# An RMSNorm-and-projection kernel: work put into the engine queues by planned times, with another load order at the start

## The chip, the cores and the metric

The kernel runs on one core of a Trainium2 chip. Its engines are TensorE (PE in the profile, with its weight loads as PEld), VectorE (DVE), ScalarE (ACT), GpSimd (POOL) and SyncE (SP), which here only issues transfers; 16 DMA engines move the data. Each engine takes its own instructions in program order. The metric is the device time of one execution in microseconds; lower is better.

## The reference

```python
# x: 8 x 1024 x 768, gamma: 768, w_qkv: 768 x 2304, all float32
rms = np.sqrt(np.mean(x ** 2, axis=-1, keepdims=True) + eps)
x_norm = x / rms * gamma
return np.matmul(x_norm, w_qkv).astype(np.float32)
```

The 8 x 1024 rows of x make 64 row tiles of 128. The output is 8192 x 2304 in float32, 75.5 MB.

## The kernel before, in words

The row factor 1/rms commutes with the product, so the kernel multiplies the raw x (as bf16) with gamma-scaled weights (as bf16) and scales each row when a result leaves PSUM. A row tile goes through: a load of 128x768 float32 (`load_x`), a cast to bf16 on VectorE (`cast_x`, L96), a transpose to the layout that TensorE wants (xT, six blocks of 128x128), the sum of squares and the square root on ScalarE (`stat`, L101 and L103) with the reciprocal on VectorE (L105), and then products. One product unit (`unit`) is six matmuls, one for each block of 128 of the 768, over up to 512 output columns into one PSUM bank, and one eviction with the row scale, on VectorE (L129) or ScalarE (L131). A full tile has units of 512, 512, 512, 512 and 256 columns: 30 matmuls and 6 x 2304 = 13,824 columns streamed.

The program has two phases.

The **head** covers row tiles 0 to 5 (`HEAD`), while the weights still arrive in nine slices of 256 columns (`load_w`, `conv_w`). The list `order` (L138) gives the order both of the loads and of the work. When a tile comes, it is cast, transposed on TensorE (`trans_pe`, L110, the two halves copied out of PSUM by VectorE L113 and ScalarE L114) and multiplied with the slices that are there; when a slice comes, its six blocks are scaled and converted by VectorE (L88) and ScalarE (L91) in turn, and all tiles that are there are multiplied with it. Code order is queue order: the conversion of the next slice stands on VectorE and ScalarE behind all evictions of the slice before it. None of the six output tiles is stored before the head's last unit is in the queues, because the stores (`store`, L134, whole rows of 2304 columns) are issued by SyncE after the loads and after the first two DMA transposes.

The **main loop** covers tiles 6 to 63. At the top of tile t it loads tile t + 6, casts tile t + 2, transposes it by DMA (`trans_dma`, L118) and takes its statistics; then come the five units of tile t and the store of its whole output. So SyncE's queue repeats: x load, transpose, store. The load of gamma is issued by ScalarE's queue behind the load of an activation table; ten matmuls on a zero tile (L150) stand on TensorE behind the transpose of gamma (L146).

Of the kernel before, what the change touches and what calls it, by code (L numbers as in the profile page):

```python
# [9 lines left out]
HEAD = 6  # L10

XBAR = True
CW = 256
# [3 lines left out]
def kernel(  # L17
# [8 lines left out]
    nc = tc.nc  # L26
# [9 lines left out]
    assert K == Kw  # L36
# [4 lines left out]
    NC = N // CW  # L41
    inv_k = 1.0 / float(K)

    singles = ctx.enter_context(tc.tile_pool(name="singles", bufs=1))
    wst = ctx.enter_context(tc.tile_pool(name="wst", bufs=NC))
# [5 lines left out]
    outp = ctx.enter_context(tc.tile_pool(name="outp", bufs=HEAD))  # L51
# [4 lines left out]

    ident_f = singles.tile([P, P], f32)
# [3 lines left out]
    eps_sb = singles.tile([P, 1], f32)  # L61
    nc.vector.memset(eps_sb, float(eps))
    warm = singles.tile([P, NT], bf16)
    nc.gpsimd.memset(warm, 0.0)

    tbl = singles.tile([P, 1], f32)
    nc.scalar.activation(out=tbl, in_=eps_sb, func=AF.Sqrt)  # L67

    g6 = singles.tile([KO, P], f32)
# [4 lines left out]
    X, XB, XT, RS, OUT, WF = {}, {}, {}, {}, {}, {}  # L74
# [5 lines left out]
    def load_w(c):  # L80
        WF[c] = wst.tile([P, KO, CW], f32, name="w_f")
        nc.sync.dma_start(out=WF[c], in_=wv[:, :, c * CW:(c + 1) * CW])

    def conv_w(c):
        for ko in range(KO):
            o = w_b[:, ko, c * CW:(c + 1) * CW]
            if ko % 2 == 0:
                nc.vector.tensor_scalar(out=o, in0=WF[c][:, ko, :], scalar1=g_sb[:, ko:ko + 1],  # L88
                                        scalar2=None, op0=mult)
            else:  # L90
                nc.scalar.activation(out=o, in_=WF[c][:, ko, :], func=AF.Copy,  # L91
                                     scale=g_sb[:, ko:ko + 1], bias=0.0)
# [5 lines left out]
    def stat(t):  # L98
# [5 lines left out]
        RS[t] = stats.tile([P, 1], f32, name="rstd")  # L104
        nc.vector.reciprocal(out=RS[t], in_=rms)  # L105

    def trans_pe(t):
        pt = psum_t.tile([P, KO, P], bf16, name="pt")
        for ko in range(KO):
            nc.tensor.transpose(out=pt[:, ko, :], in_=XB[t][:, ko * P:(ko + 1) * P], identity=ident)  # L110
# [9 lines left out]
    def unit(t, n0, nl, eng):  # L120
        pm = psum_mm.tile([P, NT], f32, name="pm")
        for ko in range(KO):
            nc.tensor.matmul(out=pm[:, :nl], lhsT=XT[t][:, ko, :], rhs=w_b[:, ko, n0:n0 + nl],  # L123
                             start=(ko == 0), stop=(ko == KO - 1))
        if t not in OUT:
            OUT[t] = outp.tile([P, N], f32, name="ot")
        o = OUT[t][:, n0:n0 + nl]
        if eng:
# [4 lines left out]
    def store(t, n0=0, nl=N):  # L133
        nc.sync.dma_start(out=of[t * P:(t + 1) * P, n0:n0 + nl], in_=OUT[t][:, n0:n0 + nl])  # L134
# [3 lines left out]
    order = [("x", 0), ("w", 0), ("x", 1), ("x", 2), ("w", 1), ("x", 3), ("w", 2),  # L138
             ("x", 4), ("x", 5)] + [("w", c) for c in range(3, NC)]
    load_x(0)  # L140
    nc.scalar.dma_start(out=g6, in_=gamma.rearrange("(ko p) -> ko p", p=P))
    for kind, i in order[1:]:
        (load_x if kind == "x" else load_w)(i)

    g_ps = psum_t.tile([P, KO], f32, name="pt")
    nc.tensor.transpose(out=g_ps, in_=g6, identity=ident_f[:KO, :KO])  # L146
    nc.vector.tensor_copy(out=g_sb, in_=g_ps)  # L147
    wps = psum_mm.tile([P, NT], f32, name="pm")
    for _ in range(10):
        nc.tensor.matmul(out=wps, lhsT=ident, rhs=warm, start=True, stop=True)  # L150

    xs, ws = [], []
    flip = 0
    for kind, i in order:
        if kind == "x":
            cast_x(i)
            trans_pe(i)
            stat(i)
            xs.append(i)
            todo = [(i, c) for c in ws]  # L160
        else:
            conv_w(i)
            ws.append(i)
            todo = [(t, i) for t in xs]
        for t, c in todo:
            unit(t, c * CW, CW, flip)
            flip ^= 1


    AHEAD = 2  # L170
    trans = trans_dma if XBAR else trans_pe
    for t in range(HEAD, min(HEAD + 6, MT)):
        load_x(t)
    for t in range(HEAD, min(HEAD + AHEAD, MT)):
        cast_x(t)
        trans(t)
        stat(t)
    for t in range(HEAD):
        store(t)
    n_tiles = [(i, min(NT, N - i)) for i in range(0, N, NT)]  # L180
    for t in range(HEAD, MT):
        a = t + AHEAD
        if t + 6 < MT:
            load_x(t + 6)
        if a < MT:
            cast_x(a)
            if XBAR:
                trans(a)
            stat(a)
        for i, (n0, nl) in enumerate(n_tiles):  # L190
            unit(t, n0, nl, i % 2 == 0)
            if i == 2 and a < MT and not XBAR:
                trans(a)
            if t == MT - 1:
                store(t, n0, nl)
# [37 lines left out]
```

## Time and profile before

| | us |
|---|---|
| runs shown | 434.64, 432.77, 434.39 (median 434.39) |
| the profiled execution | 435.1 |
| its span, from the first to the last instruction | 433.2 |
| TensorE busy in the span | 394.3 |
| VectorE busy, ScalarE busy, GpSimd busy | 175.6, 179.2, 1.2 |
| mean granted TensorE clock, as a share | 0.984 |

The span is 1.9 us shorter than the profiled execution's own time. The profile cuts the span into 40 slices of 10.8 us and gives each engine's busy share in tenths. A matmul's end is modelled and matmuls overlap, so TensorE's pace is read from starts, not from busy time. An entry of the chain of waits is one piece of the path that ended last: its start, its length, and what it was.

### The profile page before, as it was taken

The numbers are of one execution on the slowest core, as the hardware profiler recorded it, in microseconds if no ns is written. First come the engines' busy times: TensorE is split into PE (matmuls) and PEld (weight loads), VectorE is DVE, ScalarE is ACT, GpSimd is POOL, SyncE is SP. The second block draws the span as 40 slices with busy tenths as digits, with TensorE's granted clock in tenths as the row PEclk, the third lists the DMA queues.
The fourth block names the chain that finished last, engine by engine and source line by source line (L and its number), as shares of the span: only waits on it lengthen the run. The fifth ranks groups of instructions, "written<-read, shape, count | busy, mean of one in ns | idle before, by whom it ended". The sixth has DMA issues, their size and how long they took to land.

```text
span 433.2 us, 5483 instructions
## 1 busy us (share of the span) xinstructions
PE 394.3 (91%) x2076; PEld 208.7 (48%) x2111; DVE 175.6 (41%) x365; ACT 179.2 (41%) x370; POOL 1.2 (0%) x7
## 2 busy tenths in 40 slices
PE   3576888667999999999999999999999999999996
PEld 1344666232555555455555545555554555555453
DVE  1324444231444443444444344444434444443432
ACT  1445555330444443344344334434433443443431
POOL 1000000000000000000000000000000000000000
PEclk9999999696999999999999999999999999999999
DMA  8991000799999999999999999999999999999775
GB/s 299 359 368 65 3 0 2 281 402 357 291 313 286 302 305 300 310 315 314 292 295 308 301 305 314 311 279 313 304 301 309 313 307 294 300 306 300 248 244 218
DMA packets 72501, 119.50 MB, mean 276 GB/s; under 512 B 48662, under 2 KB 55708, under 8 KB 64412
## 3 DMA queue, kind: packets, MB, share of 16 engines
q1 hardware_dynamic: 72464, 119.16, 88.9%
q8 instruction: 16, 0.26, 0.2%
q14 instruction: 9, 0.07, 0.0%
q10 hardware_dynamic: 12, 0.00, 0.0%
HBM read 32.25 MB, written 75.50 MB: 249 GB/s over the span
## 4 chain that ended last, share of the span: by engine, by line
PE 87%; DMA 5%; DVE 3%; ACT 3%; issue 1%; DVEq 0%; ACTq 0%
PE pm L123 85%; DMA xT<-xb 4%; DVE ot L129 1%; DMA g<-in_gamma_dram 1%; ACT sq L101 1%; PE pm L150 1%; PE pt L110 1%; ACT xT L114 1%; DVE w_b L88 1%; DVE xT L113 1%; DVE xb L96 0%; ACT rms L103 0%; ACT L67 0%; ACT ot L131 0%; DVE rstd L105 0%
## 5 line engine op out<-in xcount | busy, mean ns | idle before, releaser
L123 PE MATMUL pm<-w_b,xT 128*128 128x512 bf16 (+1 forms) x2029 | 385.7, 350 | 24.3 <-DMA xT<-xb 10.6
L123 PEld LDWEIGHTS <-xT 128*128 128x128 bf16 x2064 | 204.0, 99 | 205.2 <-issue 12.5
L129 DVE TENSOR_SCALAR ot<-pm,rstd 128x512 f32<-128x512 f32 (+1 forms) x201 | 128.1, 638 | 213.6 <-PE pm L123 208.4
L131 ACT ACTIVATE ot<-pm,rstd 128x512 f32<-128x512 f32 (+1 forms) x143 | 92.5, 647 | 228.0 <-PE pm L123 226.8
L101 ACT ACTIVATE sq<-x_t 128x768 bf16<-128x768 f32 x64 | 53.3, 834 | 0.0
L96 DVE CAST xb<-x_t 128x768 bf16<-128x768 f32 x64 | 35.2, 549 | 0.0
L105 DVE RECIPROCAL rstd<-rms 128x1 f32<-128x1 f32 x64 | 10.5, 164 | 25.8 <-ACT rms L103 25.7
L103 ACT ACTIVATE rms<-ssq,eps_sb 128x1 f32<-128x1 f32 x64 | 18.8, 294 | 2.1
L101 ACT ACTIVATION_READ_ACCUMULATOR sq<-x_t 128x1 f32 x64 | 12.2, 191 | 0.0
L91 ACT ACTIVATE w_b<-w_f,g_sb 128x256 bf16<-128x256 f32 x27 | 11.6, 496 | 0.0
L114 ACT COPY xT<-pt 128x384 bf16<-128x384 bf16 x6 | 2.9, 480 | 19.9 <-DVE xT L113 19.9
L110 PE MATMUL pt<-ident,xb 128*128 128x128 bf16 x36 | 4.3, 280 | 4.2 <-DVE xb L96 4.2
L88 DVE TENSOR_SCALAR w_b<-w_f,g_sb 128x256 bf16<-128x256 f32 x27 | 7.8, 345 | 0.0
L146 PE MATMUL pt<-ident_f,g 6*128 6x6 f32 x1 | 0.2, 238 | 7.1 <-DMA g<-in_gamma_dram 7.1
L110 PEld LDWEIGHTS <-xb 128*128 128x128 bf16 x36 | 3.2, 127 | 6.4 <-DVE xb L96 5.7
L113 DVE COPY xT<-pt 128x384 bf16<-128x384 bf16 x6 | 2.1, 358 | 8.6 <-PE pt L110 8.6
L150 PE MATMUL pm<-warm,ident 128*128 128x512 bf16 x10 | 4.4, 628 | 0.0
L146 PEld LDWEIGHTS pt<-ident_f,g 6*128 6x128 f32 x1 | 0.2, 178 | 7.1 <-issue 7.1
L147 DVE COPY g_sb<-pt 128x6 f32<-128x6 f32 x1 | 0.2, 166 | 5.5 <-PE pt L146 5.5
L150 PEld LDWEIGHTS <-ident 128*128 128x128 bf16 x10 | 1.3, 140 | 2.3 <-issue 2.2
L67 ACT ACT_TABLE_LOAD x1 | 1.3, 1283 | 0.7 <-PEq L214 0.7
L60 DVE CAST ident<-ident_f 128x128 bf16<-128x128 f32 x1 | 0.5, 511 | 1.3 <-POOL ident_f masks.py:199 1.3
(9 smaller groups left out, 1.7 us busy)
## 6 DMA issues: line engine op xcount, KB each, us to landing
out_dram<-ot SPq DMA_DIRECT2D x63, 1152.0 KB, 5.4
x_t<-in_x_dram SPq DMA_DIRECT2D x64, 384.0 KB, 6.1
w_f<-in_w_qkv_dram SPq DMA_DIRECT2D x9, 768.0 KB, 10.6
out_dram<-ot SPq DMA_DIRECT2D x4, 256.0 KB, 2.8
xT<-xb SPq DMA_TRANSPOSE x58, 6.3
out_dram<-ot SPq DMA_DIRECT2D x1, 128.0 KB, 1.9
g<-in_gamma_dram ACTq DMA_DIRECT2D x1, 3.0 KB
```

The lines of the kernel that those rows point to most:

```text
L88: nc.vector.tensor_scalar(out=o, in0=WF[c][:, ko, :], scalar1=g_sb[:, ko:ko + 1], scalar2=None, op0=mult)
L91: nc.scalar.activation(out=o, in_=WF[c][:, ko, :], func=AF.Copy, scale=g_sb[:, ko:ko + 1], bias=0.0)
L96: nc.vector.tensor_copy(out=XB[t], in_=X[t])
L101: nc.scalar.activation(out=sq, in_=X[t], func=AF.Square, accum_out=ssq)
L103: nc.scalar.activation(out=rms, in_=ssq, func=AF.Sqrt, scale=inv_k, bias=eps_sb)
L105: nc.vector.reciprocal(out=RS[t], in_=rms)
L110: nc.tensor.transpose(out=pt[:, ko, :], in_=XB[t][:, ko * P:(ko + 1) * P], identity=ident)
L114: nc.scalar.copy(out=XT[t][:, h:, :], in_=pt[:, h:, :])
L123: nc.tensor.matmul(out=pm[:, :nl], lhsT=XT[t][:, ko, :], rhs=w_b[:, ko, n0:n0 + nl], start=(ko == 0), stop=(ko == KO - 1))
L129: nc.vector.tensor_scalar(out=o, in0=pm[:, :nl], scalar1=RS[t], scalar2=None, op0=mult)
L131: nc.scalar.activation(out=o, in_=pm[:, :nl], func=AF.Copy, scale=RS[t], bias=0.0)
L150: nc.tensor.matmul(out=wps, lhsT=ident, rhs=warm, start=True, stop=True)
```

## The change

Instead of issuing instructions as the code runs, the new program collects calls with a planned time (`at`) and issues them sorted by it. The planned time of a unit is when a running sum of matmul time says TensorE reaches it; the casts, transposes, statistics, evictions and stores get times around it. The sorted order is each engine's queue; the hardware still waits for data by semaphores, not by the planned times.

- Head: loads come in the order w x x x w x x w x w w w. The weight slices are 256, 256, 256, 512, 512 and 512 columns wide, and the third holds columns 2048 to 2303. Two buffers serve the slices of 512, so the third of them waits for the conversion of the first.
- A slice's six blocks are converted by VectorE, ScalarE and GpSimd in turn, two each.
- The load of gamma is the first instruction of the program on ScalarE's queue; the zero tile is set by VectorE; eight warm-up matmuls stand ahead of gamma's transpose and use the zero tile for both operands.
- The reciprocal is a step of its own (`recip`). The whole transposed tile is copied out of PSUM by VectorE (`copy_xT`).
- Tiles 6 to 11 are transposed on TensorE, in the stream of the tile before; DMA transposes begin with tile 12, planned 7.5 us ahead of the tile's first unit.
- The output tile is two buffers, columns 0 to 1023 and 1024 to 2303, seven of each; each half is stored as soon as it is full, in the head too. The last tile is still stored unit by unit. Evictions alternate between VectorE and ScalarE over the whole program.

```diff
-HEAD = 6
-XBAR = True
-CW = 256
+ARRIVALS = "wxxxwxxwxwww"
+C0 = [0, 256, 2048, 512, 1024, 1536]
+CHUNKS = [256, 256, 256, 512, 512, 512]
+FIRST_XBAR = 12
+WARM = 8
...
+    PARTS = [(0, 1024), (1024, N - 1024)]
...
-    outp = ctx.enter_context(tc.tile_pool(name="outp", bufs=HEAD))
+    outp = ctx.enter_context(tc.tile_pool(name="outp", bufs=7))
...
+    g6 = singles.tile([KO, P], f32)
+    nc.scalar.dma_start(out=g6, in_=gamma.rearrange("(ko p) -> ko p", p=P))
...
+        WF[c] = wst.tile([P, KO, n], f32, name=f"w_f{n}", bufs=3 if n == 256 else 2)
...
-            if ko % 2 == 0:
...
+            if ko % 3 == 0:
+                nc.vector.tensor_scalar(out=o, in0=i, scalar1=g, scalar2=None, op0=mult)
+            elif ko % 3 == 1:
+                nc.scalar.activation(out=o, in_=i, func=AF.Copy, scale=g, bias=0.0)
             else:
...
+                nc.gpsimd.tensor_scalar(out=o, in0=i, scalar1=g, scalar2=1.0, op0=mult, op1=mult)
...
+    def copy_xT(t):
         XT[t] = xTp.tile([P, KO, P], bf16, name="xT")
-        h = KO // 2
-        nc.vector.tensor_copy(out=XT[t][:, :h, :], in_=pt[:, :h, :])
-        nc.scalar.copy(out=XT[t][:, h:, :], in_=pt[:, h:, :])
+        nc.vector.tensor_copy(out=XT[t], in_=PT[t])
...
+    def store(t, h, n0, nl):
+        p0 = PARTS[h][0]
+        nc.sync.dma_start(out=of[t * P:(t + 1) * P, n0:n0 + nl], in_=OUT[t, h][:, n0 - p0:n0 - p0 + nl])
...
+    def at(time, fn, *args):
+        plan.append((time, len(plan), fn, args))
...
+            nc.tensor.matmul(out=wps, lhsT=warm[:, :P], rhs=warm, start=True, stop=True)
+
+    US = 6 * 0.2158 / 512
...
+    def unit(t, n0, nl, ready=0.0):
+        s = max(state["pe"], ready)
+        state["pe"] = e = s + nl * US
+        at(s, mm, t, n0, nl)
+        state["flip"] ^= 1
+        at(e + 0.2, evac, t, n0, nl, state["flip"])
+        h = part(n0)
+        left[t, h] = left.get((t, h), PARTS[h][1]) - nl
+        if t == MT - 1:
+            at(e + 0.9, store, t, h, n0, nl)
+        elif left[t, h] == 0:
+            at(e + 1.4, store, t, h, *PARTS[h])
+
+    at(0.0, warm_up)
+    at(3.0, gamma_in)
...
+            now += 1.02
+            at(now, cast_x, t)
+            at(now + 0.6, trans_pe, t)
+            at(now + 1.0, copy_xT, t)
+            at(now + 0.1, stat, t)
+            at(now + 1.6, recip, t)
...
+                unit(t, C0[c], CHUNKS[c], now + 1.7)
...
     for t in range(HEAD, MT):
...
+        T = state["pe"]
+        at(T - 15, load_x, t)
+        if t < FIRST_XBAR:
+            at(T - 4.5, cast_x, t)
+            at(T - 3.0, trans_pe, t)
+            at(T - 2.5, copy_xT, t)
+        else:
+            at(T - 8.5, cast_x, t)
+            at(T - 7.5, trans_dma, t)
+        at(T - 5, stat, t)
+        at(T - 3, recip, t)
+        for n0, nl in n_tiles:
+            unit(t, n0, nl)
+
+    for _, _, fn, args in sorted(plan, key=lambda p: p[:2]):
+        fn(*args)
```

VectorE at the start, before (xb_148 and xb_182 are the casts of tiles 0 and 1; w_f_106 is the first weight slice):

```order
L113 COPY xT_157<-pt_150 128x384
L105 RECIPROCAL rstd_165<-rms_163 128x1
L88 TENSOR_SCALAR w_b_102<-w_f_106,g_sb_101 128x256 x3
L96 CAST xb_182<-x_t_108 128x768
L113 COPY xT_191<-pt_184 128x384
L105 RECIPROCAL rstd_199<-rms_197 128x1
L129 TENSOR_SCALAR ot_208<-pm_201,rstd_199 128x256
```

VectorE at the start, after (xb_146, xb_162 and xb_187 are the casts of tiles 0, 1 and 2; w_f256_104 and w_f256_112 are the first two slices):

```order
L94 TENSOR_SCALAR w_b_103<-w_f256_104,g_sb_102 128x256 x2
L102 CAST xb_146<-x_t_106 128x768
L124 COPY xT_160<-pt_153 128x768
L102 CAST xb_162<-x_t_108 128x768
L114 RECIPROCAL rstd_169<-rms_151 128x1
L124 COPY xT_185<-pt_171 128x768
L102 CAST xb_187<-x_t_110 128x768
L146 TENSOR_SCALAR ot0_194<-pm_178,rstd_169 128x256
L114 RECIPROCAL rstd_196<-rms_167 128x1
L124 COPY xT_212<-pt_198 128x768
L114 RECIPROCAL rstd_216<-rms_192 128x1
L94 TENSOR_SCALAR w_b_103<-w_f256_112,g_sb_102 128x256 x2
```

The first slice's conversion moved ahead of the first cast, and the casts of tiles 1 and 2 ahead of the first eviction.

TensorE at the start, after: the end of tile 1's transpose (xb_162), the first unit, and the beginning of tile 2's transpose (xb_187). Before, the first unit stood directly behind the transpose of tile 0.

```order
L120 MATMUL pt_153<-ident_100,xb_146 128x128
L120 LDWEIGHTS xb_162
L120 MATMUL pt_171<-ident_100,xb_162 128x128
...
L133 LDWEIGHTS xT_160
L133 MATMUL pm_178<-w_b_103,xT_160 128x256
...
L120 LDWEIGHTS xb_187
L120 MATMUL pt_198<-ident_100,xb_187 128x128
```

The first unit moved behind the transposes of two tiles.

SyncE in the steady part, before: two turns of the loop (x_t is the load of tile t + 6, xT the transpose of tile t + 2, ot the store of tile t).

```order
L78 DMA x_t_1344<-in_x_dram 128x768
L118 DMA_TRANSPOSE xT_1348<-xb_1346 128x6x128
L134 DMA out_0_dram<-ot_1364 128x2304
L78 DMA x_t_1399<-in_x_dram 128x768
L118 DMA_TRANSPOSE xT_1403<-xb_1401 128x6x128
L134 DMA out_0_dram<-ot_1419 128x2304
```

SyncE in the steady part, after (ot0 is the first half of an output tile, ot1 the second half of the same tile; the transpose between them is that of the tile two behind it):

```order
L83 DMA x_t_1193<-in_x_dram 128x768
L152 DMA out_0_dram<-ot0_1191 128x1024
L128 DMA_TRANSPOSE xT_1217<-xb_1205 128x6x128
L152 DMA out_0_dram<-ot1_1215 128x1280
L83 DMA x_t_1250<-in_x_dram 128x768
L152 DMA out_0_dram<-ot0_1248 128x1024
L128 DMA_TRANSPOSE xT_1274<-xb_1262 128x6x128
L152 DMA out_0_dram<-ot1_1272 128x1280
```

The transpose moved from behind an x load and a whole store to behind the store of half a tile, and nearer to the tile that needs it.

## Rows read from the trace of the kernel before

**Rows 1.** The page: busy time by engine, then tenths in 40 slices.

```profile
PE 394.3 (91%) x2076; PEld 208.7 (48%) x2111; DVE 175.6 (41%) x365; ACT 179.2 (41%) x370; POOL 1.2 (0%) x7
...
PE   3576888667999999999999999999999999999996
...
GB/s 299 359 368 65 3 0 2 281 402 357 291 313 286 302 305 300 310 315 314 292 295 308 301 305 314 311 279 313 304 301 309 313 307 294 300 306 300 248 244 218
```

**Rows 2.** Chain of waits, steady part: start us, us, what.

```profile
131.03 9.46 PE pm L123 x49
...
160.20 9.46 PE pm L123 x49
```

**Rows 3.** Chain of waits, start, loop entry and end.

```profile
1.91 5.07 DMA g<-in_gamma_dram
...
76.38 2.85 DMA xT<-xb
...
86.50 14.01 DMA xT<-xb
...
429.90 0.48 DVE ot L129
```

**Rows 4.** Timeline of TensorE, head and loop entry: start us, us, what [idle before].

```profile
14.96 1.44 PE L123 MATMUL pm<-w_b,xT 128*128 128x256 bf16 x6 [2.60 <-DVE w_b L88]
...
24.52 3.79 PE L123 MATMUL pm<-w_b,xT 128*128 128x256 bf16 x17 [0.34 <-ACT w_b L91]
29.35 0.82 PE L110 MATMUL pt<-ident,xb 128*128 128x128 bf16 x6 [1.04 <-DVE xb L96]
...
34.20 2.87 PE L123 MATMUL pm<-w_b,xT 128*128 128x256 bf16 x24 [0.84 <-DVE w_b L88]
38.12 0.51 PE L110 MATMUL pt<-ident,xb 128*128 128x128 bf16 x6 [1.05 <-DVE xb L96]
...
71.19 4.18 PE L123 MATMUL pm<-w_b,xT 128*128 128x256 bf16 x36 [0.84 <-DVE w_b L88]
...
100.56 9.68 PE L123 MATMUL pm<-w_b,xT 128*128 128x512 bf16 x36 [6.66 <-DMA xT<-xb]
```

**Rows 5.** Windows: busy us by engine, then PEclk, DMA share, GB/s.

```profile
103.00:106.00 3.00, 3.00 (x10) 1.14 (x9) 0.75 (x1) 0.27 (x1) 0.00 (x0) 0.60 1.10 376
106.00:109.00 3.00, 3.00 (x19) 1.62 (x18) 0.77 (x2) 1.10 (x3) 0.00 (x0) 1.00 1.12 354
```

**Rows 6.** The first x load: issue time, then landing.

```profile
L78 SPq DMA_DIRECT2D x_t<-in_x_dram x1: 402/402/402, 0.7 to 0.7; - x1
...
DMA to landing us min/median/max: 3.1/3.1/3.1
```

**Rows 7.** The first weight load: issue time, then landing.

```profile
L82 SPq DMA_DIRECT2D w_f<-in_w_qkv_dram x1: 419/419/419, 1.2 to 1.2; - x1
...
DMA to landing us min/median/max: 5.1/5.1/5.1
```

**Rows 8.** Groups by shape: xcount | busy us, mean ns | idle before.

```profile
L129 DVE TENSOR_SCALAR ot<-pm,rstd 128x512 f32<-128x512 f32 x116 | 87.0, 750 | 120.5 <-PE pm L123 115.6 <-DMA out_dram<-ot 4.9
...
L129 DVE TENSOR_SCALAR ot<-pm,rstd 128x256 f32<-128x256 f32 x85 | 41.1, 484 | 93.1 <-PE pm L123 92.7
L96 DVE CAST xb<-x_t 128x768 bf16<-128x768 f32 x64 | 35.2, 549 | 0.0
...
L88 DVE TENSOR_SCALAR w_b<-w_f,g_sb 128x256 bf16<-128x256 f32 x27 | 7.8, 345 | 0.0
...
L113 DVE COPY xT<-pt 128x384 bf16<-128x384 bf16 x6 | 2.1, 358 | 8.6 <-PE pt L110 8.6
```

**Rows 9.** Timeline of GpSimd at the start.

```profile
1.01 0.29 POOL masks.py:199 TENSOR_SCALAR_AFFINE_SELECT ident_f<-ident_f 128x128 f32<-128x128 f32 x1
```

**Rows 10.** Timeline of SyncE, steady part.

```profile
203.80 2.59 SPq L118 DMA_TRANSPOSE xT<-xb  x1
```

**Rows 11.** The tile xT between 150 and 200 us.

```profile
DMA to landing us min/median/max: 6.2/6.5/8.5
```

More of the change, by code (lines that the diff above doesn't have):

```diff
@@ L35 @@
     Kw, N = w_qkv.shape
-    assert K == Kw
+    assert K == Kw and sum(CHUNKS) == N
     P = 128
@@ L55 @@
     ctx.enter_context(tc.manual_schedule())
+    g6 = singles.tile([KO, P], f32)
+    nc.scalar.dma_start(out=g6, in_=gamma.rearrange("(ko p) -> ko p", p=P))
+    eps_sb = singles.tile([P, 1], f32)
+    nc.vector.memset(eps_sb, float(eps))
+    warm = singles.tile([P, NT], bf16)
+    nc.vector.memset(warm, 0.0)
+    tbl = singles.tile([P, 1], f32)
+    nc.scalar.activation(out=tbl, in_=eps_sb, func=AF.Sqrt)
     ident_f = singles.tile([P, P], f32)
@@ L131, in unit @@
             nc.scalar.activation(out=o, in_=pm[:, :nl], func=AF.Copy, scale=RS[t], bias=0.0)
[L133 to L154, printed above, removed]
-        if kind == "x":
[L156 to L160, printed above, removed]
-        else:
[L162 to L167, printed above, removed]
@@ L170 @@
[L170 to L179, printed above, removed]
+    def store(t, h, n0, nl):
+        p0 = PARTS[h][0]
+        nc.sync.dma_start(out=of[t * P:(t + 1) * P, n0:n0 + nl], in_=OUT[t, h][:, n0 - p0:n0 - p0 + nl])
+    plan = []
+    def at(time, fn, *args):
+        plan.append((time, len(plan), fn, args))
@@ new lines, in gamma_in, with warm_up @@
+    def gamma_in():
+        g_ps = psum_t.tile([P, KO], f32, name="pt")
+        nc.tensor.transpose(out=g_ps, in_=g6, identity=ident_f[:KO, :KO])
+        nc.vector.tensor_copy(out=g_sb, in_=g_ps)
+    def warm_up():
+        wps = psum_mm.tile([P, NT], f32, name="pm")
+        for _ in range(WARM):
+            nc.tensor.matmul(out=wps, lhsT=warm[:, :P], rhs=warm, start=True, stop=True)
+    US = 6 * 0.2158 / 512
+    left = {}
+    state = {"pe": 0.0, "flip": 0}
+    def unit(t, n0, nl, ready=0.0):
[4 more added lines that the diff above has]
+        at(e + 0.2, evac, t, n0, nl, state["flip"])
+        h = part(n0)
+        left[t, h] = left.get((t, h), PARTS[h][1]) - nl
[3 more added lines that the diff above has]
+            at(e + 1.4, store, t, h, *PARTS[h])
@@ new lines @@
+    at(0.0, warm_up)
+    at(3.0, gamma_in)
+    now, xs, ws = 2.3, [], []
+    for n, kind in enumerate(ARRIVALS):
+        if kind == "x":
+            t = len(xs)
+            at(0.1 * n - 9, load_x, t)
+            now += 1.02
[4 more added lines that the diff above has]
+            at(now + 1.6, recip, t)
+            xs.append(t)
+            for c in ws:
+                unit(t, C0[c], CHUNKS[c], now + 1.7)
+        else:
+            c = len(ws)
+            at(0.1 * n - 9, load_w, c)
+            now += CHUNKS[c] * (2.45 / 256 if CHUNKS[c] == 256 else 4.1 / 512)
+            at(now, conv_w, c)
+            ws.append(c)
+            for t in xs:
+                unit(t, C0[c], CHUNKS[c], now + 1.0)
```

68 lines of the change are left out of this document (24 added, 44 removed).

## The prediction

> **What bounds the kernel now.** I read the page first, then the chain of waits in order of time, then TensorE's timeline of the head, and last the transfers.
>
> The page shows two different kernels in one span [rows 1]. From slice 10 on TensorE is busy 9 tenths and more to the end. In the seven slices before 76 us it stands at 3 to 8, and in the last four of these the DMA engines move 65, 3, 0 and 2 GB/s: the loads are in, and no store has been issued. So the late part is bound by TensorE and the early part is not.
>
> The pace of the late part is in the chain: three pieces fill the 29.17 us from 131.03 to 160.20 [rows 2]. That is five tiles, 5.834 us each; 13,824 columns at that pace are 0.422 ns each, which is one column per cycle of the 2.4 GHz level. Nothing in the change shortens a matmul, so 64 tiles cost 64 x 5.834 = 373.4 us before and after. The span of 433.2 us is 59.8 us longer than this. These 59.8 us are what there is to win, and they lie in four places:
>
> - The first unit starts at 14.96 us [rows 4]. The gamma load, issued at 1.91 us, took 5.07 us [rows 3], because it queued among the bulk loads, and warm-up, casts and conversion stood behind it.
> - In the head the stream of matmuls has holes. Late in the head a slice gives 36 matmuls in 4.18 us and then TensorE waits 0.84 us for the next conversion, which stands behind the evictions [rows 4]. Early in the head the holes are longer.
> - The array ran at half its clock in the early head: 17 matmuls of 256 columns in 3.79 us, 0.22 us each, against 24 in 2.87 us, 0.12 each, from 34.20 us on [rows 4]. These are the 1.2 and the 2.4 GHz levels.
> - At the entry of the main loop the chain is on two DMA transposes, 2.85 and 14.01 us [rows 3]. The second sits in the queue behind six whole-row stores. TensorE starts again at 100.56 us [rows 4], and the clock is at its lower level: 0.60 on average from 103 to 106 us, 1.00 after that [rows 5].
>
> Behind the last matmul stands a tail of 433.2 - 429.9 = 3.3 us: an eviction of 0.48 us and the last store [rows 3].
>
> **The change part by part.**
>
> *Start.* The first x load was issued at 0.7 us and landed 3.1 us later, the first weight slice at 1.2 + 5.1 = 6.3 us [rows 6, 7]: 2.5 us behind it. The loads move at 360 to 370 GB/s [rows 1], so a 0.39 MB tile is about 1.05 us and a slice of 0.79 MB 2.1 to 2.5. With the slice first it lands near 5.25 us and tile 0 near 6.3. The gamma load is now the first thing that ScalarE issues; if it still took 5.07 us it would land at 5.8, half a microsecond behind the slice. VectorE then casts tile 0 (0.55 us [rows 8]) to 6.85. TensorE transposes it: a group of six took 0.82 us at the low clock with its modelled end [rows 4], about 0.65 until the next engine can start, so 7.5. The whole-tile copy costs between one and two of the half copies of 0.358 us [rows 8]; I take 0.6, so 8.1. The sorted order puts the cast and transposes of tile 1 ahead of the first unit: 0.55 + 0.65 more. The first unit starts at 9.3 us. Bounds: 8.1 if the second transpose hides, 10.5 if gamma is late as well.
>
> *Clock.* Dense work that began at 100.56 us ran at the low level until 105.4: the mean of 0.60 over 3 us is 2.4 us at half and 0.6 at full [rows 5]. That is 4.8 us after its start. The same 4.8 us from 9.3 us on cost 2.4 us of work. Lower bound 0, if the warm-up matmuls already raise the clock. Upper bound from the head before, where the clock was low until about 34 us [rows 4]: (34 - 9.3) / 2 = 12.4 us. I take 2.4, because from 9.3 us on two or more tiles' units and transposes are queued at any time, as at 100.56, and not one as at 14.96.
>
> *Transposes on TensorE.* Twelve groups of six now stand in the stream; two are over before the first unit. The ten others cost at least 768 columns at the pace of the stream, 0.32 us, and at most the 0.51 us of a whole group at full clock [rows 4]. At 0.35 that is 3.5 us (3.2 to 5.1).
>
> *Conversions and holes of the head.* Units of 256 columns take 0.65 us at full clock, so after the first three slices TensorE has 18 units (11.7 us) and four groups of transposes (1.4) and is busy until about 9.3 + 2.4 + 11.7 + 1.4 = 24.8 us. The first slice of 512 lands, after 6.3 MB, near 20 us and is converted by 22 to 23. The second has landed by 24.5. The third must wait until the first is converted, and lands near 31, ten microseconds before TensorE needs it. So from 20 us on loads and conversions are covered by queued matmuls. Before that VectorE is the tight engine: 6 casts, 6 copies, 6 conversions and 9 evictions are 3.3 + 3.6 + 2.1 + 4.4 = 13.4 us [rows 8], of the 19.5 between 5.3 and 24.8. GpSimd's conversion is in no row. Its lower bound is VectorE's 0.345 us for 256 columns [rows 8]; the nearest row of GpSimd, 0.29 us for 128 columns [rows 9], gives 0.6 and 1.2 us for 256 and 512. The two of a slice then end 1.2 us after it lands. For all holes of the head after the first unit I take 1.0 us, between 0 and 3.6 (three times 1.2, if every early conversion is waited for in full).
>
> *Loop entry.* The transposes of tiles 6 to 11 no longer pass through SyncE, and the half stores go out from about 27 us on, while the DMA engines before stood still. The two waits of 2.85 and 14.01 us go. What is late next would be an x load behind the head's stores: tile 6's is queued behind five half stores, must land by 44 us, and some 6 us of stores stand in front of it. That is covered.
>
> *Steady part.* The bytes for a tile are the same. A DMA transpose took 2.59 us to issue [rows 10] and 6.5 us (6.2 to 8.5) to land [rows 11]; before, it had nearly two tiles, 11 us. Now it is issued 7.5 us ahead of its use, behind half a store instead of a whole store and a load. I cost it at nothing: 1.0 us of cover is left at the old median, more if the shorter queue counts.
>
> *Sum.* 373.4 + 9.3 (start) + 2.4 (clock) + 3.5 (transposes) + 1.0 (holes) + 3.3 (tail) = 392.9 us of span, against 433.2. The profiled execution was 435.1 for its span of 433.2, 1.9 more: 394.8. The median of the runs is 0.7 below that execution: **394 us**.
>
> **One rule weighed.** VectorE's cast and conversion from SBUF to SBUF run at about 0.40 ns a column ((549 - 345) / 512), its evictions from PSUM at 1.04 ((750 - 484) / 256) [rows 8]; so the two forms go through VectorE at different rates. The Trainium skill, page "SBUF — State Buffer", section "Who interferes with whom", says that casts and scalar multiplies of VectorE in a two-port mode share a port pair with GpSimd, and that whichever starts first holds it for its whole instruction. No run here shows it yet. By that rule the twelve GpSimd conversions stop VectorE's casts and conversions while they run; it is the second rival.
>
> **Rivals.**
>
> *The clock rises late.* For it: before, it stayed low for 19 us after the first unit. Against it: the holes that stood there are filled. Halfway to the bound of 12.4 us the sum grows by 5: 399 us.
>
> *GpSimd holds up VectorE.* Each of the first three slices then costs VectorE two GpSimd conversions of 0.6 us, 3.6 us in the stretch where VectorE is the tight engine; the three later slices are covered. 394 + 3.6 = 398 us. For it: casts are queued right behind the conversion. Against it: a cast of 0.55 us also fits between two conversions.
>
> *Transposes late in some tiles.* The maximum of 8.5 us [rows 11] is 1.0 over the lead. If one tile in five is so late, 52 / 5 x 1.0 = 10 us: 404.
>
> *Slower: transposes late in every tile.* Place: the wait of each tile from 12 on for its xT, 52 of them. If landing costs 8.5 us in each, as in the worst row, TensorE stops 1.0 us a tile: 394 + 52 = 446 us. It decides against the change from 0.78 us a tile on (40.4 / 52), a landing of 8.3 us. For it: the lead shrank from about 11 to 7.5 us, and a load or a store may still be in front. Against it: the median is 6.5, with more bytes ahead in the queue than there will be; and a stopped TensorE makes no stores, which empties the queue.
>
> **How the numbers follow.** The forecast has 0.68, with its own range of 389 to 398 us: downwards the clock term of 2.4 and 1 to 2.5 us of start and holes, upwards the upper ends of transposes and holes. The late clock has 0.10 (399), the held-up VectorE 0.12 (398), some late transposes 0.06 (404), all late 0.03 (446); 0.01 is left. The range runs from 389 to 404: it takes in the first three rivals and leaves out the slower case, the part of the late clock above 404 us, and a start faster than I see. About 0.5% is what a measurement of this kernel can tell from no change. All cases but one lie far on the faster side: faster 0.96, same 0.01, slower 0.03.
>
> **What would show it.** The first unit near 9.3 us. Matmuls of 256 columns 0.22 us apart until about 14 us and 0.11 after that. Tile 6's first unit near 9.3 + 35 + 2.4 + 1.4 (four groups of transposes) + 1 = 49 us, where it was 79. No wait of TensorE for xT, and 5.83 us a tile in the steady part. DMA engines that are busy from 35 to 76 us. GpSimd conversions of 0.4 to 1.2 us; longer ones, or casts well over 0.55 us, speak for the port. The forecast is wrong if the steady part has a wait a tile, or if tile 6 starts later than 55 us.

## The result, and the profile after the change

| | before | after |
|---|---|---|
| median of four runs, us | 433.58 | 394.60 |
| lowest and highest, us | 432.69, 434.64 | 393.88, 394.80 |
| span of the profiled execution, us | 433.2 | 392.1 |
| mean granted TensorE clock | 0.984 | 0.994 |

The ratio is 0.910, with a 95% interval of 0.907 to 0.913: 39 us faster at the medians. The forecast was 394 us. The spans differ by more, 41.1 us, because the profiled execution before took 435.1 us, longer than the four timed ones, and the one after is the shortest of its four; the other three after have spans of 392.7 to 393.0.

The page after, with the lines of [rows 1] and the granted clock in tenths; a slice is 9.8 us.

```profile
PE 383.7 (98%) x2037; PEld 197.0 (50%) x2037; DVE 158.1 (40%) x319; ACT 182.8 (47%) x369; POOL 8.0 (2%) x18
...
PE   5999999999999999999999999999999999999996
...
PEclk9899999999999999999999999999999999999999
...
GB/s 273 381 283 405 241 396 257 289 274 303 318 299 296 286 327 292 326 291 285 342 288 311 309 263 339 310 295 312 298 304 295 308 315 298 298 317 293 303 260 192
```

TensorE is at 9 tenths from the second slice to the last but one, and the stretch without transfers before 76 us is filled. The path is in the chain of waits (start us, us, what):

```profile
1.25 5.41 DMA x_t<-in_x_dram
...
6.69 0.69 DVE xb L102
...
9.88 1.28 PE pm L133 x6
11.16 0.66 PE pt L120 x6
11.82 0.75 PE pm L133 x6
...
12.60 0.47 ACT ot L148
13.07 0.41 ACT w_b L96
...
13.51 0.79 PE pm L133 x5
...
20.26 25.30 PE pm L133 x138
45.57 0.34 PE pt L120 x6
45.90 6.47 PE pm L133 x30
...
77.39 311.22 PE pm L133 x1602
388.63 0.47 ACT ot L148
```

From 13.51 us to the last matmul TensorE alone is on the path, but for 0.04 us. The chain has no wait for an xT; before, two of these stood on it [rows 3]. The timeline of TensorE gives the warm-up, the first transposes and the first unit:

```profile
1.22 3.59 PE L169 MATMUL pm<-warm 128*128 128x512 bf16 x8 [1.22 <-DVE warm L67]
...
7.43 0.51 PE L120 MATMUL pt<-ident,xb 128*128 128x128 bf16 x6 [2.42 <-DVE xb L102]
...
9.67 1.49 PE L133 MATMUL pm<-w_b,xT 128*128 128x256 bf16 x6
```

By the chain, the transposes of tile 6 end at 45.90 us; two units of the head (12 matmuls of 512 columns, 0.2155 us apart) are still ahead of it, so its first unit starts at 48.5 us. Before, it started at 79.28 us:

```profile
79.28 0.61 PE L123 MATMUL pm<-w_b,xT 128*128 128x512 bf16 x1 [3.92 <-DMA xT<-xb]
```

With these marks the 41.1 us of span divide by stretch: 14.96 - 9.67 = 5.3 us came before the first unit, 64.3 - 38.8 = 25.5 from there to tile 6, and 350.6 - 340.1 = 10.5 from tile 6 to the last matmul; the tail grew by 0.2. The pace of the steady part is the old one. A part of the middle stretch is clock: inside their groups, the matmuls of 256 columns start about 0.21 us apart until 33.0 us before (48 of them) and until 11.9 us after (7 of them). Some forty matmuls at 0.10 us more each are up to 4 us; no run separates these from the holes.

### The profile page after: what moved, and what is told of

The parts are those of the page before. It is cut to its first block, busy times and chain, and to the rows that moved or that the text cites. A ratio compares the mean times of both kernels' runs of the same rounds, so it can differ in the third digit from the quotient of the medians.

```text
span 392.1 us, 5550 instructions
## 1 busy us (share of the span) xinstructions
PE 383.7 (98%) x2037; PEld 197.0 (50%) x2037; DVE 158.1 (40%) x319; ACT 182.8 (47%) x369; POOL 8.0 (2%) x18
## 4 chain that ended last, share of the span: by engine, by line
PE 97%; DMA 1%; DVE 0%; ACT 0%; SPq 0%; issue 0%
PE pm L133 95%; DMA x_t<-in_x_dram 1%; PE pt L120 1%; DVE xb L102 0%; ACT ot L148 0%; DVE xT L124 0%; SPq L88 0%; ACT w_b L96 0%
## 5 line engine op out<-in xcount | busy, mean ns | idle before, releaser
L133 PE MATMUL pm<-w_b,xT 128*128 128x512 bf16 (+1 forms) x1956 | 376.4, 355 | 0.1
L133 PEld LDWEIGHTS <-xT 128*128 128x128 bf16 x1956 | 191.2, 98 | 181.4 <-issue 0.3
L146 DVE TENSOR_SCALAR ot<-pm,rstd 128x512 f32<-128x512 f32 (+1 forms) x163 | 112.2, 689 | 215.0 <-PE pm L133 200.5
L148 ACT ACTIVATE ot<-pm,rstd 128x512 f32<-128x512 f32 (+1 forms) x163 | 103.8, 637 | 199.6 <-PE pm L133 138.9
L124 DVE COPY xT<-pt 128x768 bf16<-128x768 bf16 x12 | 6.7, 557 | 10.6 <-PE pt L120 10.3
L120 PE MATMUL pt<-ident,xb 128*128 128x128 bf16 x72 | 6.7, 235 | 3.6 <-DVE xb L102 3.5
L96 ACT ACTIVATE w_b<-w_f,g_sb 128x256 bf16<-128x256 f32 (+1 forms) x12 | 6.7, 605 | 3.3 <-DMA w_f<-in_w_qkv_dram 3.3
L98 POOL TENSOR_SCALAR w_b<-w_f,g_sb 128x256 bf16<-128x256 f32 (+1 forms) x12 | 7.3, 623 | 23.9 <-DMA w_f<-in_w_qkv_dram 23.9
L94 DVE TENSOR_SCALAR w_b<-w_f,g_sb 128x256 bf16<-128x256 f32 (+1 forms) x12 | 4.9, 453 | 0.6 <-DMA w_f<-in_w_qkv_dram 0.6
L169 PE MATMUL pm<-warm 128*128 128x512 bf16 x8 | 3.6, 630 | 1.2 <-DVE warm L67 1.2
```

The costliest lines, as they stand in the source:

```text
L94: nc.vector.tensor_scalar(out=o, in0=i, scalar1=g, scalar2=None, op0=mult)
L96: nc.scalar.activation(out=o, in_=i, func=AF.Copy, scale=g, bias=0.0)
L98: nc.gpsimd.tensor_scalar(out=o, in0=i, scalar1=g, scalar2=1.0, op0=mult, op1=mult)
L120: nc.tensor.transpose(out=PT[t][:, ko, :], in_=XB[t][:, ko * P:(ko + 1) * P], identity=ident)
L124: nc.vector.tensor_copy(out=XT[t], in_=PT[t])
L133: nc.tensor.matmul(out=PM[t, n0][:, :nl], lhsT=XT[t][:, ko, :], rhs=w_b[:, ko, n0:n0 + nl], start=(ko == 0), stop=(ko == KO - 1))
```

## The experiments

The twelve runs were timed in other sessions than the pair above, so each ratio is taken to the kernel before in its own session (medians 432.6 to 433.8). A comparison with the changed kernel's 394.6 us goes across sessions. The first five and the last two start from the changed kernel, the other five from the kernel before.

### DMA transposes from tile 6 on

```diff
-FIRST_XBAR = 12
+FIRST_XBAR = 6
```

> The changed kernel, but tiles 6 to 11 are transposed by DMA like the rest (36 transposes fewer on TensorE). Theory 1 (once the head's stores go out early and in halves, the queue in front of a DMA transpose is short): no new wait for xT, and the six groups of 0.34 us fall out, 394.6 - 2.0 = 392.6 us. Rival (the TensorE transposes of tiles 6 to 11 are needed, since the head's stores and the x loads still fill the queue between 36 and 66 us): waits for xT of 1 us or more at several of these tiles, 395 us or more.

Measured 393.6 us, ratio 0.909 (0.906 to 0.911). It lies between the two theories, and its interval contains the changed kernel's ratio. The six groups left the stream, 2.0 us, but 0.8 us came back as waits. Chain of waits and view of waits (us in total, times, longest) of this run:

```profile
60.08 6.80 DMA xT<-xb
```

```profile
PEld L133 <- DMA xT<-xb: 1.1, 2, 0.7
PE pm L133 <- DMA xT<-xb: 0.5, 1, 0.5
```

Two tiles started late, the worse behind a landing of 6.80 us; by the starts of their matmuls they cost 0.6 and 0.2 us. So the transposes of tiles 6 to 11 on TensorE cost 2.0 us and save 0.8 of it. The span is only 0.4 us shorter than the changed kernel's, because in this trace the warm-up did not raise the clock, and the last transposes of the head end 0.6 us later (20.86 against 20.26). Tile 0's transposes took 0.82 us here, not 0.51:

```profile
7.19 0.82 PE L120 MATMUL pt<-ident,xb 128*128 128x128 bf16 x6 [2.18 <-DVE xb L102]
```

### Conversions without GpSimd

```diff
-            if ko % 3 == 0:
+            if ko % 2 == 0:
...
-            elif ko % 3 == 1:
-                nc.scalar.activation(out=o, in_=i, func=AF.Copy, scale=g, bias=0.0)
             else:
-                nc.gpsimd.tensor_scalar(out=o, in0=i, scalar1=g, scalar2=1.0, op0=mult, op1=mult)
+                nc.scalar.activation(out=o, in_=i, func=AF.Copy, scale=g, bias=0.0)
```

> The changed kernel, but the weights are converted by VectorE and ScalarE alone (three blocks of a slice each), GpSimd idle. Theory 1 (after 12 us the conversions are covered by queued matmuls, and the shared port costs only the 0.14 us by which the first cast is longer): within 0.5 us of 394.6. Rival 1 (the third engine is what shortens the head): 2 us slower or more. Rival 2 (GpSimd holds VectorE up in the head): 1 us faster or more.

Measured 394.5 us, ratio 0.910 (0.908 to 0.913): no difference from the changed kernel. The third engine brings nothing that can be measured, and costs nothing. So none of the gain comes from the number of engines; what the place of the conversions in the queues is worth is tried below.

### Whole-row stores

```diff
-    PARTS = [(0, 1024), (1024, N - 1024)]
+    PARTS = [(0, N)]
```

> The changed kernel, but an output tile is one buffer and is stored in whole rows of 2304 columns, so the head's six stores can only start when the last slice is multiplied, near 42 us. Theory 1 (TensorE-bound, the x loads have slack): within 1 us of 394.6; DMA engines idle from 32 to 42 us without effect. Rival (the early half stores are a main part of the gain, as the burst of six whole stores was in front of the transpose that cost 14 us before): waits for x_t or xT after 42 us, 400 us or more.

Measured 394.1 us, ratio 0.911 (0.908 to 0.914): the same. The bandwidth by slice shows a dip and a crowd where the first stores start late, 112 and then 408 and 416 GB/s:

```profile
GB/s 276 381 280 112 226 408 416 359 270 331 301 318 287 306 327 287 295 324 267 328 320 281 316 326 275 310 308 287 318 312 306 290 310 319 288 301 272 332 262 241
```

The crowd made VectorE wait for x loads, but never TensorE. Splitting the stores was worth nothing in time. It did shorten the landing of the transposes, which here is, from 150 to 350 us:

```profile
DMA to landing us min/median/max: 3.5/4.9/6.4
```

In the same stretch the median is 4.2 us with the split and 6.3 before. So of the 2.1 us a third comes with the halves, and with them the transpose's place behind a half store. The rest came with the planned times. In this run SyncE still issues store, x load, transpose, as before, but the transpose comes 1.8 to 3.0 us behind the load (the first two lines), where it came 0.5 us behind it (the third line, and [rows 10]):

```profile
202.91 0.43 SPq L83 DMA_DIRECT2D x_t<-in_x_dram  x1
204.66 1.42 SPq L128 DMA_TRANSPOSE xT<-xb  x1
...
203.28 0.42 SPq L78 DMA_DIRECT2D x_t<-in_x_dram  x1
```

### The lead of the DMA transposes, 4.0 us and 5.0 us

```diff
-            at(T - 7.5, trans_dma, t)
+            at(T - 4.0, trans_dma, t)
```

> The changed kernel with the DMA transposes planned 4.0 us instead of 7.5 us ahead of the tile's first unit; in SyncE's order they then stand behind the second half store of the tile two before it. The landing in the changed kernel is 4.1 to 4.6 us. Theory 1 (the slower rival of the prediction: what lands late is paid in each of 52 tiles): 0.3 to 1.0 us a tile, 410 to 445 us, with TensorE waiting for xT about 52 times. Rival (a stopped TensorE makes stores later and so empties the queue, which pays for itself): within 3 us of 394.6.

Measured 399.7 us, ratio 0.923 (0.920 to 0.926): 5 us more, between the two theories. The chain of waits has seven landings in it, of which these are the first and the last:

```profile
80.46 5.54 DMA xT<-xb
...
358.72 5.25 DMA xT<-xb
```

The view of the tile xT over the steady part (70 to 385 us) says why it is seven and not 52:

```profile
DMA to landing us min/median/max: 3.6/4.2/5.5
```

The lead, from a transpose's issue to the first matmul that uses it, was 4.3 to 5.6 us in this run, 4.7 in the median. Only the late landings, of 4.85 us and more, stopped TensorE: seven times for 0.3 to 0.9 us, and twice for less than 0.2. After five of these seven the next transpose, issued before TensorE stopped, landed with about 1 us to spare. So with the median landing under the lead, lateness costs by the tail of the landings, 4.6 us in all, and not by the number of tiles.

With T - 5.0 in the same line:

> The changed kernel with the DMA transposes planned 5.0 us ahead of the tile's first unit instead of 7.5; in SyncE's order they still stand between the two half stores. Theory 1 (what matters is where the transpose stands among the stores, and its landing of 4.1 to 4.6 us is still inside 5.0): within 1 us of 394.6, no wait for xT. Rival (2.5 us of lead are 2.5 us of lateness): waits in most of the 52 tiles, 400 us or more.

Measured 394.4 us, ratio 0.909 (0.905 to 0.913): no difference. SyncE's order of instructions is the same as with 7.5, and so are the lead (median 7.5 us) and the landing (4.2 us) in its trace. The planned time only sorts: a lead changes when an instruction passes another one in the queue.

### Before, with TensorE transposes for tiles 6 to 11

```diff
-        trans(t)
+        trans_pe(t)
...
-            if XBAR:
-                trans(a)
+            if a >= 12:
+                trans_dma(a)
...
-            if i == 2 and a < MT and not XBAR:
-                trans(a)
+            if i == 2 and a < 12:
+                trans_pe(a)
```

> The kernel before with one part of the change: tiles 6 to 11 are transposed on TensorE, DMA transposes from tile 12; head and stores as before. Theory 1 (the loop entry is worth what its waits and its two stretches at the lower clock cost, about 10 to 13 us of the 41): 420 to 424 us, tile 6 starts about 77 us, no wait for xT. Rival (the six whole-row stores keep the loop entry slow in another way, by output buffers that come free late): a wait for output buffers takes the place, 428 us or more.

Measured 425.5 us, ratio 0.981 (0.977 to 0.985): 8.3 us less, between the theories. The waits for DMA transposes at the loop entry are gone, but others stand there (timeline of TensorE):

```profile
74.30 0.51 PE L110 MATMUL pt<-ident,xb 128*128 128x128 bf16 x6 [1.05 <-DVE xb L96]
77.59 0.51 PE L110 MATMUL pt<-ident,xb 128*128 128x128 bf16 x6 [2.78 <-DVE xb L96]
```

The casts now are late, because in this program's order they stand behind the head's evictions on VectorE. Taking the slow transposes out is half a step; in the changed kernel the casts stand earlier, and no such wait is left at the loop entry.

### Before, with gamma loaded first

```diff
+    g6 = singles.tile([KO, P], f32)
+    nc.scalar.dma_start(out=g6, in_=gamma.rearrange("(ko p) -> ko p", p=P))
...
-    g6 = singles.tile([KO, P], f32)
...
-    nc.scalar.dma_start(out=g6, in_=gamma.rearrange("(ko p) -> ko p", p=P))
```

> The kernel before with one part of the change: the gamma load is the first instruction on ScalarE's queue. Theory 1 (the first unit comes 3 to 4 us earlier, near 11 us, and the head behind it is a chain of in-order work that keeps the gain): 429 to 431 us. Rival (the head waits for weight slices later on anyway): within 1 us of 433.6.

Measured 428.4 us, ratio 0.988 (0.983 to 0.992): 5.4 us less, more than expected.

```profile
9.15 1.44 PE L124 MATMUL pm<-w_b,xT 128*128 128x256 bf16 x6 [2.60 <-DVE w_b L89]
```

The first unit came 5.8 us earlier than in [rows 4], and none of it was lost later. That start varies by itself: in two runs with the load of gamma in its old place it was 14.04 and 13.64 us. One line moved gives about as much as the whole stretch before the first unit gained in the change.

### Before, with later conversions ahead of the products

```diff
-    for kind, i in order:
+    done = set()
+    for n, (kind, i) in enumerate(order):
...
-            conv_w(i)
+            for c in (i, i + 1):
+                if c not in done and (c == i or order[n + 1:n + 2] == [("w", c)]):
+                    conv_w(c)
+                    done.add(c)
```

> The kernel before with the conversion of slices 4 to 8 put into the queues ahead of the products (and so of the evictions) of the slice before it, as the planned times do. Nothing else is changed. Theory 1 (queue order alone makes the holes of 0.84 us): 5 x 0.84 = 4.2 us faster, 429.4 us, 36 matmuls in 4.2 us without a hole from slice 4 on. Rival (the holes come from what the conversions cost, and VectorE and ScalarE would be late somewhere else): less than 1.5 us faster.

Measured 427.7 us, ratio 0.985 (0.981 to 0.989): 6.1 us less, where the idle times of 0.84 us made 4.2.

```profile
44.07 23.83 PE L123 MATMUL pm<-w_b,xT 128*128 128x256 bf16 x216 [0.84 <-DVE w_b L88]
```

Six slices in one row. The size was misread: a slice came every 5.02 us [rows 4: 71.19, and five like it], and 36 matmuls 0.11 us apart start within 3.9 to 4.0, so each hole was near 1.1 us. The 0.84 is counted from a modelled end that lies behind the next possible start. Five holes at 1.08 are 5.4 us; the two traces agree, as the first of the six slices starts 2.05 us earlier than before (44.07 against 46.12) and tile 6 starts 7.49 us earlier. The remaining 0.7 has no cause in the edit that the trace shows; it is no more than executions of the kernel before differ by.

### Before, with preparation one item ahead

```diff
-    for kind, i in order:
+    def prep(n):
+        kind, i = order[n]
...
+        else:
+            conv_w(i)
+
+    prep(0)
+    for n, (kind, i) in enumerate(order):
+        if n + 1 < len(order):
+            prep(n + 1)
+        if kind == "x":
...
-            conv_w(i)
```

> The kernel before, but in the head the preparation of each item of the load list (cast, transposes and statistics of a tile, or the conversion of a slice) is put into the queues ahead of the products of the item in front of it. Same loads, same slices of 256, no GpSimd, whole-row stores at the end of the head. Theory 1 (most of the head's 25 us were queue order: 5.4 us of holes behind late slices, and in the early head 21 us more than in the changed kernel for the same 18 units): 15 to 20 us faster, 414 to 419 us. Rival (the early head was short because VectorE and ScalarE had too much to do for nine narrow slices, and wide slices and GpSimd are what helped): only the holes of the late slices go, 5 to 8 us faster, 426 to 429 us.

Measured 421.7 us, ratio 0.974 (0.972 to 0.977): 10.9 us less, short of the 15 to 20.

```profile
14.42 0.82 PE L110 MATMUL pt<-ident,xb 128*128 128x128 bf16 x6 [3.60 <-DVE xb L96]
...
18.02 0.82 PE L110 MATMUL pt<-ident,xb 128*128 128x128 bf16 x6 [1.50 <-DVE xb L96]
...
34.02 27.67 PE L123 MATMUL pm<-w_b,xT 128*128 128x256 bf16 x252
```

The late head is one stream of 252 matmuls; the early head still waits for casts, and the granted clock is 0.50 from 13.0 to 26.6 us. What holds the casts shows in the next run.

### Before, with the three edits together

The edits of the last section, of gamma and of tiles 6 to 11 in one kernel; the lines are those above.

```diff
+    nc.scalar.dma_start(out=g6, in_=gamma.rearrange("(ko p) -> ko p", p=P))
...
+            prep(n + 1)
...
+            if i == 2 and a < 12:
+                trans_pe(a)
```

> The kernel before with three single edits at once: preparation one item ahead in the head, the gamma load first, and tiles 6 to 11 transposed on TensorE. Loads, slices, engines of the conversion and whole-row stores as before. Theory 1 (these three make the gain, the new load order, wide slices, GpSimd and half stores add little): the single gains add up, 433.6 - 5.4 - 8.3 - 17 = 403 us, within 3 us. Rival (they overlap, or the parts left out carry the rest): 410 us or more.

Measured 410.5 us, ratio 0.948 (0.946 to 0.951): 22.1 us less, where the three alone sum to 24.6. The rival was right: 16 us to the changed kernel remain. By the traces, 11.62 - 9.67 = 2.0 us of them lie before the first unit, 49.9 - 38.8 = 11.1 between it and tile 6 (61.54 us here), and 2.3 behind. VectorE's timeline and the view of waits show the early head:

```profile
13.93 0.17 DVE L106 RECIPROCAL rstd<-rms 128x1 f32<-128x1 f32 x1 [1.71 <-ACT rms L104]
14.01 0.54 DVE L97 CAST xb<-x_t 128x768 bf16<-128x768 f32 x1
```

```profile
DVE rstd L106 <- ACT rms L104: 28.6, 64, 1.7
```

A reciprocal of 0.17 us waits 1.71 us for ScalarE, which copies, squares and takes the root for the same tile first; the next tile's cast stands behind it, and TensorE's transposes wait for that cast. In the changed kernel the reciprocal is a step of its own, queued later, and its group by shape shows no idle time:

```profile
L114 DVE RECIPROCAL rstd<-rms 128x1 f32<-128x1 f32 x64 | 9.8, 153 | 0.0
```

Not all of the 11.1 us lies in the early head. As in the run with TensorE transposes alone, tiles 6 and 7 wait for late casts at the loop entry, 4.2 us by the starts, and behind it the granted clock is 0.50 from 61.8 to 65.2 us, which costs 1.7 of the 2.3:

```profile
61.20 0.51 PE L111 MATMUL pt<-ident,xb 128*128 128x128 bf16 x6 [2.78 <-DVE xb L97]
```

The other 6.9 us are the early head, where the granted clock is 0.50 from 11.0 to 17.4 us. How they divide between the wait for the root, the clock, the order of loads and the wider slices was not tried by a run of its own and stays open.

### After, with work between the first transposes

```diff
-    def warm_up():
+    def warm_up(n=WARM):
...
-        for _ in range(WARM):
+        for _ in range(n):
...
+    at(3.1, warm_up, 5)
+    at(6.5, warm_up, 2)
```

The added matmuls multiply the zero tile; their product is not used.

> The changed kernel with five more matmuls on the zero tile behind gamma's transpose and two more between the transposes of tiles 0 and 1, where TensorE waited 2.4 and 1.1 us. Theory 1 (the clock fell at 8.4 us because TensorE had little to do from 5.0 us on, and the units from 9.7 to 11.9 us ran at half pace): the clock stays up from 5 us, 1.1 us less, 393.5 us. Rival (the head waits for conversions at 12.6 to 13.5 us anyway, and a faster start only makes that hole longer): within 0.4 us of 394.6.

Measured 393.1 us (392.9 to 393.3), ratio 0.908 (0.906 to 0.910). The median is 1.5 us under the changed kernel's, the span 1.0, by the ratios it is 0.7 us; the two ratios' intervals overlap, so the time alone doesn't settle it. The trace shows what changed (windows: busy us by engine, PEclk, DMA share, GB/s). The changed kernel:

```profile
5.10:8.40 3.30, 0.51 (x6) 0.34 (x6) 2.07 (x5) 2.59 (x6) 1.10 (x2) 1.00 1.03 397
8.50:11.80 3.30, 2.74 (x19) 2.15 (x20) 2.15 (x7) 1.69 (x6) 0.82 (x2) 0.50 1.07 375
11.90:15.00 3.10, 2.94 (x27) 2.06 (x26) 2.16 (x7) 2.37 (x7) 0.01 (x1) 1.00 1.07 362
```

With the bridge, windows and then the timeline of TensorE:

```profile
5.10:8.40 3.30, 3.04 (x13) 0.90 (x11) 2.29 (x6) 2.81 (x7) 1.12 (x2) 1.00 1.03 393
8.50:11.80 3.30, 2.51 (x26) 1.86 (x27) 2.63 (x10) 1.61 (x6) 0.94 (x2) 1.00 1.07 376
```

```profile
4.95 2.28 PE L169 MATMUL pm<-warm 128*128 128x512 bf16 x5
...
9.17 0.82 PE L133 MATMUL pm<-w_b,xT 128*128 128x256 bf16 x6
10.46 0.51 PE L120 MATMUL pt<-ident,xb 128*128 128x128 bf16 x6 [0.47 <-DVE xb L102]
```

In the changed kernel the warm-up had raised the clock, and it fell again, to the 1.2 GHz level, after a stretch in which TensorE worked 0.51 of 3.30 us. With the stretch filled, the units from 9.17 us on run at 2.4 GHz. But the clock did not stay up from 5 us, as was expected: the five added matmuls start 0.43 us apart, half the pace, and only from 7.2 us on is the pace the full one. (PEclk reads 1.00 ahead of the first change that a trace records; there the starts decide.) Of the 1.0 us of span, 0.5 lies before the first unit, where the x load also came 0.2 us earlier, and 0.5 behind it. What the first unit itself gains is lost to a wait for a cast: from its start to the next transposes it is 1.29 us, against 1.33.

The rise by the warm-up is not certain either. With the same head, the clock was up at 5.0 to 5.5 us and down from 8.4 to 8.9 us in four traces (the changed kernel, whole rows, both leads), and rose for the first time at 13.5 and 12.8 us in the two others (DMA transposes from tile 6 on, conversions without GpSimd). In both traces with the bridge it was up by 7.1 us and did not fall again before the end.

### The best of the pieces

The bridge, and

```diff
-            at(now, conv_w, c)
+            at(now - (1.0 if c == 1 else 0.0), conv_w, c)
...
-        at(T - 15, load_x, t)
+        at(T - (20 if t < FIRST_XBAR else 15), load_x, t)
...
-            at(T - 4.5, cast_x, t)
-            at(T - 3.0, trans_pe, t)
-            at(T - 2.5, copy_xT, t)
+            at(T - 11.0, cast_x, t)
+            at(T - 10.0, trans_dma, t)
```

> The changed kernel with the extra zero matmuls of the run before, the second slice's conversion planned 1 us earlier, and tiles 6 to 11 transposed by DMA with a planned lead of 10 us and x loads 20 us ahead. Theory 1 (the gains add: 2.0 us of transposes without the 1.0 us of lateness seen with a lead of 7.5, 1.1 us of clock, up to 0.9 us of hole): 390.6 to 391.6 us. Rival (earlier x loads and transposes collide with the head's stores or hold up VectorE's evictions behind a cast that waits): 393 us or more.

Measured 391.2 us (391.1 to 391.7), ratio 0.904 (0.902 to 0.906): faster than both kernels, than the changed one by 3.4 us at the medians and 2.6 by the ratios, with intervals that don't meet.

```profile
9.84 0.82 PE L133 MATMUL pm<-w_b,xT 128*128 128x256 bf16 x6
...
19.76 80.46 PE L133 MATMUL pm<-w_b,xT 128*128 128x256 bf16 x411
```

No transpose and no wait breaks the stream from 19.76 us on. The six groups are worth 6 x 0.34 = 2.0 us when the DMA transposes of these tiles get loads and leads that cover the crowded stretch, as they had not in the first experiment. The earlier conversion gave nothing: from the first unit to the last transposes' end it is 9.92 us, as with the bridge alone (9.17 to 19.09), since a wait for a cast took the place of the conversion's.

## Why the prediction was right, step by step

*The pace of 373.4 us.* Right; the chain has 1602 matmuls in 311.22 us, with no wait in them.

*Start, 9.3 us.* 9.67. The x load landed at 6.66 us, where 6.3 was forecast. The order was right: two groups of transposes stand before the first unit. The load of gamma was over by 4.7 us, when its transpose starts behind the warm-up, and not at 5.8.

*Clock, 2.4 us.* Mis-sized: 1.0 us by the starts. The forecast took the delay of a rise from the loop entry [rows 5]. In fact the warm-up raised the clock at 5.0 us; it fell at 8.45 and rose at 11.86. In that time six matmuls took 1.28 us instead of 0.65, and a group of transposes 0.66 instead of 0.34; the bridge brings both to the full pace, though a wait for a cast takes the first unit's gain. The matmuls were 0.21 us apart until 11.9 us, and not until 14. The term is no fixed size: in the two traces where the warm-up did not raise the clock it is larger, and the profiled execution is the fastest of its four.

*Transposes, 3.5 us.* 3.4: by the starts a group takes 0.34 us of the stream at full pace. The chain shows 4.0 for the ten groups, with the low clock and modelled ends in it.

*Holes of the head, 1.0 us.* 0.9 by the starts, in six holes between 10.7 and 16.1 us. On the chain an eviction of ScalarE and, behind it, the conversion of the second slice fill 12.57 to 13.51, but TensorE still had matmuls for most of that; the hole behind it is 0.27 us. The next two, 0.22 and 0.14, end right behind casts (14.29 and 16.09 us). The size came out right; the places had not been named, and moving one conversion could not win more than a part.

*Loop entry.* Right: tile 6's first unit at 48.5 us, forecast 49. The tiles 6 to 11 needed no slow transpose, and the casts that were late in the run on the kernel before were early here. The forecast called the two transfers of 2.85 and 14.01 us waits; TensorE stood 3.92 us at the first (the line of 79.28 us above) and 6.66 us at the second [rows 4]. No term of the sum used them.

*Steady part.* Right, with more room than thought. A transpose took 1.6 us to issue and landed in 4.2 us in the median, against 2.59 and 6.5 [rows 10, 11]; the run with whole rows says that the planned times did more for it than the shorter stores. Over tiles 12 to 63:

```profile
DMA to landing us min/median/max: 3.2/4.2/5.8
```

*Tail, 3.3 us.* 3.5.

The sum is 373.4 + 9.7 + 1.0 + 3.4 + 0.9 + 3.5 = 391.9, against 392.1 of span and 392.9 forecast. The clock's error of -1.4 was met by errors of +0.4 and +0.2 in others, so the total is better than its terms: that part of the agreement is luck.

*The rivals.* The late clock did not happen in this trace; the latest first rise in any trace with this head was at 13.5 us. The port rule did, at a price of 0.14 us on the path. The timelines of GpSimd and of VectorE after:

```profile
5.86 1.10 POOL L98 TENSOR_SCALAR w_b<-w_f,g_sb 128x256 bf16<-128x256 f32 x2 [4.55 <-DMA w_f<-in_w_qkv_dram]
```

```profile
6.69 0.68 DVE L102 CAST xb<-x_t 128x768 bf16<-128x768 f32 x1
...
8.45 0.55 DVE L102 CAST xb<-x_t 128x768 bf16<-128x768 f32 x1
```

The first cast met GpSimd's second conversion and took 0.68 us; the one that met none took 0.55. In the run without GpSimd conversions the first cast took 0.56:

```profile
6.73 0.56 DVE L100 CAST xb<-x_t 128x768 bf16<-128x768 f32 x1
```

The rival supposed two whole conversions of stop for each slice, 3.6 us; the engines met for fractions of one. The Trainium skill, page "SBUF — State Buffer", section "Who interferes with whom", says that of a VectorE cast or scalar multiply in a two-port mode and a GpSimd instruction, the one that comes second is blocked for the whole instruction of the first. The trace agrees in kind: the cast started 0.27 us before GpSimd's end and lost 0.14. So the cost here is set by how much of the first instruction is still to come, and not by the whole of it.

The slower rival priced a late landing times 52 tiles. In the run with a real lead of 4.7 us against landings of 4.2 in the median, only the tail was late, in 9 of 52 tiles, and the cost was 5 us; a price for every tile would have been wrong there. No run had its median landing above the lead, which is what the rival supposed, so what that costs is not shown.

## What to carry to other kernels

Count what the bound engine must do at its best pace, list every stretch in which it doesn't, and price a change by the stretches it fills; here a sum of six such terms held to 0.2%, with some luck in it. In a queue, look for a short instruction that waits for another engine: what stands behind it (here a cast behind a reciprocal) pays for the wait. Where stretches were idle, look at the clock behind them too. A planned time in such a program only sorts; before costing a lead, read which instructions it passes, and then compare it with the slowest landings and not with their median.

## What the runs showed of the hardware

- GpSimd converts 128x256 elements in 0.48 us and 128x512 in 0.69 us when undisturbed, against 0.34 and 0.48 on VectorE and 0.50 and 0.71 on ScalarE; where GpSimd and VectorE overlapped, GpSimd took up to 0.77 for 128x256, and VectorE up to 0.57 for 128x256 and 0.75 for 128x512 (all from the trace after).
- After the same eight warm-up matmuls, the clock was up at about 5 us in four traces and not before 12.8 us in two. Where it was up, it did not last over a stretch with 0.51 us of work in 3.30; with seven more matmuls on zeros it was up by 7.1 us and stayed up, in two traces.
- An idle time that follows matmuls in the timeline is too short by about 0.2 us: 0.84 shown, 1.00 from starts (1.11 between starts that are 0.11 apart in the stream).
- With the same bytes per tile, a DMA transpose landed in 6.3 us in the median when it was issued 0.5 us behind an x load, in 4.9 when it was issued 1.8 to 3.0 us behind it, and in 4.2 behind the store of half a tile.
